# A differential-attention block on one core: the heads' norm factors go through TensorE transposes instead of DRAM, and GpSimd computes them

## The chip, the cores and the metric

The kernel runs on one core of one Trainium2 chip. The metric is its device time in microseconds (us): of one run, from start to end on the chip. A core has five engines that each work through an instruction queue of their own in order: TensorE (PE, whose weight loads are listed as PEld), VectorE (DVE), ScalarE (ACT), GpSimd (POOL) and SyncE (SP), which here mostly issues DMAs. They wait for each other by semaphores.

## The reference, cut to what matters

One layer of a hybrid block on a sequence of 1024 rows of 1024 values: a normalised input is projected, one branch is an mLSTM, the other a differential attention of 8 heads; both are gated, projected, mixed and added. The change touches the end of the attention. Of head `h`:

```python
p = jax.nn.softmax(scores, axis=-1)
p_diff = p[:, :, 0] - lam * p[:, :, 1]
att = jnp.einsum('bhqk,bkhd->bqhd', p_diff, v)
...
att = rmsnorm(att, da_subln_g[layer]) * (1.0 - lambda_init)
y_b = att.reshape(B, S, DA_WIDTH).astype(x.dtype) * jax.nn.silu(b_z)
```

`rmsnorm` divides each row (a query position) by the root of the mean square of its 128 values. So there is one factor per head and row, 1024 factors per head.

## The kernel before, in words

All products are made in parts: each fp32 operand is split into a high and a low part (`wH`, `wL`, `hH`, `hL`, `pH`, `pL`), and three products are summed. The program runs through an opening, the mLSTM's projections, the attention, the mLSTM and the output passes. In the attention, a head has eight blocks of 128 query rows, numbered `t`:

- `scores` (line 906 on): PE writes two score maps of 128x1024 into the S banks (L919). DVE takes the negative maximum `nm` (L922), ACT the exponentials `e` with their sums `Z` (L924), DVE combines the two (`r`, `e`, L928 to L930).
- `transposes` (T): PE turns the 128x128 blocks of `e` four at a time into the one T bank (L131, a helper that records every transpose), ACT copies the high part `pH` out (L943), DVE the low part `pL` (L944). Then the bank is free again.
- `pv` (PV): 12 products per unit of `pH`, `pL` with `vH`, `vL` (L955), two units per pair of blocks; ACT copies the result, transposed (128 features by 256 rows), to `att` (L957).
- `squares` (M): two transposes of `att` into the PV bank; ACT sums the squares into `ms`, a column per block (L967). After the fourth, that is, at the end of a head, DVE and GpSimd compute the factors `rs`, 128 rows by 8 blocks: `zz` (L971), then the helper `rsqrt` (L141 to L146), in which GpSimd takes the power -0.5 (L142) and DVE the rest with one Newton step, and a last scaling (L973). The tiles have the names `rb_v`, `rb_y`, `rb_w`. GpSimd multiplies `att` with the gate `g` (tile `zg`, L976).
- `finish` (F) and `spread`: `att` has features on its partitions and rows along the free axis, so a row's factor has to be there for all partitions. PE turns `rs` into 8x128 (L131, PV bank), ACT copies it to a tile `rb` (L986), SP stores it to DRAM (`rsd`, L988) and loads it back to all 128 partitions for four blocks (512 rows) at a time (`rb`, L994).
- `scale` (G): DVE multiplies `zg` with the gain and `rb` (L998), SP stores the result (`yb`, L999). G of the first half starts the spread of the second.

While PE works on these, it has other products to fill in: the projections of the next head (`da_proj`: rotary queries and keys, `pj`, L424, whose results go through DVE (L847 to L859), GpSimd (L860 to L864), ACT (L863) and a trip through DRAM, `stk` (L868), into `qq` and `kst` (L870), which the next head's scores read), the gate `z` (L876, L877), the value projections (L446, with `vH`, `vL`, L898 and L899) and gate columns. Their weights `raw` are loaded by SP, cast by ACT (L188, L199) and split by GpSimd (L189, L204).

Who comes when on PE is set by the `Weaver`: it takes units of work from two lists, the attention's units of a head in the order of `da_cycle` and the filling projections, and puts next the unit that can start first by an estimated clock. Units say which others must have ended and how long before (`after`, with the numbers of `LAG` in us), and how long they hold a bank (`hold`). PE's order is kept as written; the other engines' orders are made from it by a scheduler at build time. `z`'s last piece of each half waits in this estimate for G of the head before, since `zg` has two buffers.

## Time and profile before

| | before |
|---|---|
| median of three runs | 1824.18 us (1822.41 to 1827.65) |
| the profiled execution | 1825.16 us |
| its span, first to last instruction | 1823.1 us |
| granted TensorE clock, mean over the span | 0.968 |
| instructions | 25192 |
| matmuls | 9375 |

A row of the busy times gives for each engine the us in which it worked, its share of the span and the count of its instructions. A row of waits reads: engine and line that waited, who ended the wait, us in total, how often, the longest. A row of the timeline reads: start (us from the span's start), duration, engine, line, operation, out<-in, shapes, count, and in brackets the engine's idle time before it and what ended that. `SPq` is a DMA's issue in SP's queue, not its transfer. A matmul's duration includes its way through the array, and matmuls overlap: what one costs PE is the distance between two starts.

### The profile page before, as it was taken

The page shows a single profiled execution, that of the slowest core. Times are in us where ns is not written, and L with a number is a line of the kernel's source. Part 1 is how long each engine was busy: PE and PEld are TensorE (multiplying, and loading weights), DVE is VectorE, ACT ScalarE, POOL GpSimd, SP SyncE. Part 2 cuts the span into 40 slices and gives each one's busy share as a digit, 9 for nine tenths or more (in the row PEclk, how much of TensorE's full clock was granted, in tenths as well). Part 3 has the DMA queues.
Part 4 walks back from the last instruction along what each step waited for, and adds up shares of the span by engine and source line. Part 5 has one row for each costly group of instructions (what it writes and reads, how often), then busy time and mean ns, then how long its engine had stood idle before and what let it go on. Part 6 is the DMA issues. An engine that isn't in the chain of part 4 may idle for free. (4 is left out here: it accounts for less than half of the span.)

```text
span 1823.1 us, 25192 instructions
## 1 busy us (share of the span) xinstructions
PE 1680.3 (92%) x9375; PEld 1398.9 (77%) x9375; DVE 1008.8 (55%) x1855; ACT 781.3 (43%) x1562; POOL 591.3 (32%) x608
## 2 busy tenths in 40 slices
PE   7999999999997978989797979999999989999998
PEld 5787887878776856777576757779989977788887
DVE  5687778751765646555564645522666663216533
ACT  6455555441543434443343435432556554213211
POOL 4866676643313122312231231122123212122100
PEclk9999999999998998989898989999999999999999
DMA  5343443533224113220322132226454426534222
GB/s 172 89 130 116 150 135 117 156 114 116 87 87 133 31 41 121 86 76 15 124 72 91 36 106 73 64 64 202 153 158 143 141 74 208 167 106 160 97 83 87
DMA packets 184973, 199.77 MB, mean 110 GB/s; under 512 B 11225, under 2 KB 134514, under 8 KB 184850
## 3 DMA queue, kind: packets, MB, share of 16 engines
q1 hardware_dynamic: 183938, 196.58, 34.3%
q8 instruction: 73, 1.20, 0.3%
q10 hardware_dynamic: 912, 1.59, 0.2%
q14 instruction: 50, 0.41, 0.1%
HBM read 135.08 MB, written 63.05 MB: 109 GB/s over the span
## 5 line engine op out<-in xcount | busy, mean ns | idle before, releaser
L424 PE MATMUL pj<-hH,wH 128*128 128x512 f32 x640 | 270.5, 423 | 3.8 <-DVE hl L859 1.9
L424 PE MATMUL pj<-hH,wL 128*128 128x512 f32 x640 | 254.4, 397 | 1.8 <-POOL wL L202 1.8
L424 PE MATMUL pj<-hL,wH 128*128 128x512 f32 x640 | 254.1, 397 | 0.2 <-DVE hL L575 0.2
L924 ACT ACTIVATE e<-S,nm 128x1024 f32<-128x1024 f32 x128 | 143.0, 1117 | 138.5 <-DVE nm L922 137.8
L204 POOL TENSOR_TENSOR wL<-raw,wH 128x1024 fp32r<-128x1024 f32 x41 | 101.1, 2465 | 307.4 <-ACT wH L199 293.8
L131 PE MATMUL T<-ident,e 128*128 128x128 f32 x512 | 83.0, 287 | 93.3 <-DVE pL L944 93.1
L944 DVE TENSOR_TENSOR pL<-T,pH 128x512 fp32r<-128x512 f32 x128 | 88.1, 688 | 135.2 <-ACT pH L943 134.8
L922 DVE TENSOR_REDUCE nm<-S 128x1 f32<-128x1024 f32 x128 | 150.5, 1218 | 20.1 <-PE S L919 19.0
L424 PEld LDWEIGHTS pj<-hH,wH 128*128 128x128 f32 x640 | 123.4, 193 | 41.6 <-issue 16.9
L446 PE MATMUL pj<-wH,hH 128*128 128x256 f32 x512 | 150.5, 294 | 0.3
L131 PEld LDWEIGHTS T<-ident,e 128*128 128x128 f32 x512 | 62.1, 146 | 115.3 <-DVE pL L944 107.7
L446 PE MATMUL pj<-wL,hH 128*128 128x256 f32 x512 | 145.5, 284 | 1.4 <-POOL wL L202 1.4
L424 PEld LDWEIGHTS pj<-hH,wL 128*128 128x128 f32 x640 | 122.6, 191 | 31.1 <-POOL wL L202 3.2
L446 PE MATMUL pj<-wH,hL 128*128 128x256 f32 x512 | 145.2, 284 | 0.0
L424 PEld LDWEIGHTS pj<-hL,wH 128*128 128x128 f32 x640 | 123.6, 193 | 20.0 <-DVE hL L575 0.6
L424 PE MATMUL pj<-sl_yb,wH 128*128 128x512 f32 x384 | 121.9, 397 | 4.4 <-ACT sl_yb L1326 1.9
L943 ACT CAST pH<-T 128x512 fp32r<-128x512 f32 x128 | 74.9, 585 | 108.3 <-PE T L131 107.1
L919 PE MATMUL S<-kst,qq 64*128 64x512 f32 x768 | 119.9, 448 | 0.2 <-ACT e L924 0.2
L189 POOL TENSOR_TENSOR wL<-raw,wH 128x512 fp32r<-128x512 f32 x32 | 41.3, 1303 | 205.4 <-ACT wH L188 194.0
L199 ACT CAST wH<-raw 128x1024 fp32r<-128x1024 f32 x56 | 58.8, 1050 | 106.6 <-PE pj L424 92.0
L446 PEld LDWEIGHTS pj<-wH,hH 128*128 128x128 f32 x512 | 98.7, 193 | 4.9 <-issue 3.9
L446 PEld LDWEIGHTS pj<-wL,hH 128*128 128x128 f32 x512 | 98.3, 192 | 2.3 <-POOL wL L202 2.3
(357 smaller groups left out, 4168.3 us busy)
## 6 DMA issues: line engine op xcount, KB each, us to landing
raw<-in_w_in_dram SPq DMA_DIRECT2D x88, 512.0 KB
stk<-hl SPq DMA_DIRECT2D x64, 256.0 KB
qq<-stk SPq DMA_DIRECT2D x16, 512.0 KB
kst<-stk SPq DMA_DIRECT2D x16, 512.0 KB
x<-in_x_dram SPq DMA_DIRECT2D x8, 512.0 KB
cak<-y SPq DMA_DIRECT2D x16, 256.0 KB
cakH<-cin SPq DMA_DIRECT2D x16, 256.0 KB
cakL<-tz SPq DMA_DIRECT2D x16, 256.0 KB
```

What stands on the lines that cost most here:

```text
L131: self.t.transpose(out, in_, self.ident[0:k, 0:k])
L189: self.p.tensor_tensor(out=vw(wL), in0=src, in1=vw(wHf), op=ALU.subtract)
L199: self.a.copy(wH, raw)
L204: self.p.tensor_tensor(out=wL, in0=raw, in1=wHf, op=ALU.subtract)
L424: self.t.matmul(ps, lhsT=l[:, k, :], rhs=r, start=(n == 0), stop=(n == 23))
L446: self.t.matmul(ps[:, i, :], lhsT=l, rhs=r[:, k, :], start=(kh == 0 and k == 0 and m == 0), stop=(kh == 1 and k == 3 and m == 2))
L919: self.t.matmul(ps[:, o], lhsT=qq[r, x, c], rhs=k[r, y, o], start=(m == 0), stop=(m == 2))
L922: v.tensor_reduce(out=nm, in_=ps, axis=AX.X, op=ALU.max, negate=True)
L924: a.activation(out=e, in_=ps, func=AF.Exp, bias=nm[:, 0:1], accum_out=Z[:, j, t:t + 1])
L943: a.copy(pH[:, :, s], ps)
L944: v.tensor_tensor(out=pL[:, :, s], in0=ps, in1=pH[:, :, s].bitcast(F32), op=ALU.subtract)
```

## The change

The trip through DRAM goes: `finish` and `spread` are removed, and with them the unit F, the tile `rb` and its DMAs. Instead `scale` (G) becomes a unit of PE that takes the T bank. For each of its four blocks it transposes one column of `rs`, read 128 times over by a broadcast access pattern, so that the 128 factors of the block stand along the free axis on every partition. DVE multiplies from that bank. The whole chain of `rs` is done by GpSimd, where a fused multiply-add of two tensors becomes two instructions. In `da_cycle` G moves from t = 4 and 6 to t = 4 and 5. In `LAG`, F is now how long G comes after the last M (6.0), and G, the time from G to the last piece of `z`, is 6.0 for both halves (it was 18.9 and half of that). The end of the last head is woven anew with one unit less.

```diff
-LAG = dict(Th=2.2, Sh=5.0, PVh=3.7, Mh=8.1, Fh=5.0, qk=14.0, T=6.8, PV=3.7, M=4.5, F=0.4, TTh=1.9, TT=3.2, POh=1.6,
-           PO=1.7, Wh=0.3, W=2.0, STh=2.1, ST=4.9, th=1.8, t=4.1, aq=9.0, outh=6.6, out=14.0, G=18.9)
+LAG = dict(Th=2.2, Sh=5.0, PVh=3.7, Mh=8.1, qk=14.0, T=6.8, PV=3.7, M=4.5, F=6.0, TTh=1.9, TT=3.2, POh=1.6,
+           PO=1.7, Wh=0.3, W=2.0, STh=2.1, ST=4.9, th=1.8, t=4.1, aq=9.0, outh=6.6, out=14.0, G=6.0)
...
-    def rsqrt(self, pool, ssq, scale, bias, name, bufs=1):
+    def rsqrt(self, pool, ssq, scale, bias, name, bufs=1, eng=None):
...
+        v = eng or self.v
...
-            self.v.scalar_tensor_tensor(out=val, in0=ssq, scalar=scale, in1=bias, op0=ALU.mult, op1=ALU.add)
+            if eng is None:
+                v.scalar_tensor_tensor(out=val, in0=ssq, scalar=scale, in1=bias, op0=ALU.mult, op1=ALU.add)
+            else:
+                v.tensor_scalar(out=val, in0=ssq, scalar1=scale, scalar2=None, op0=ALU.mult)
+                v.tensor_tensor(out=val, in0=val, in1=bias, op=ALU.add)
         self.p.tensor_tensor(out=y, in0=val, in1=self.mhalf[:, 0:shp[1]], op=ALU.pow)
-        self.v.tensor_tensor(out=w, in0=y, in1=y, op=ALU.mult)
+        v.tensor_tensor(out=w, in0=y, in1=y, op=ALU.mult)
...
-            z[(half + 1) * self.PIECES - 1].after = ((("G", h - 1, half), LAG["G"] / (half + 1)),)
+            z[(half + 1) * self.PIECES - 1].after = ((("G", h - 1, half), LAG["G"]),)
...
-                v.scalar_tensor_tensor(out=zz, in0=Z0, scalar=EPS, in1=Z0, op0=ALU.mult, op1=ALU.mult)
-                rs = self.rsqrt(w1, st["ms"], 1.0 / 128.0, zz, "rb")
-                v.tensor_scalar(out=rs, in0=rs, scalar1=(1.0 - LAMBDA_INIT) * 0.5, scalar2=None, op0=ALU.mult)
+                p.tensor_scalar(out=zz, in0=Z0, scalar1=EPS, scalar2=None, op0=ALU.mult)
+                p.tensor_tensor(out=zz, in0=zz, in1=Z0, op=ALU.mult)
+                rs = self.rsqrt(w1, st["ms"], 1.0 / 128.0, zz, "rb", eng=p)
+                p.tensor_scalar(out=rs, in0=rs, scalar1=(1.0 - LAMBDA_INIT) * 0.5, scalar2=None, op0=ALU.mult)
...
-        def finish():
-
-            rs = st["rs"]
-            ps = self.bank("PV")
-            self.tr(ps[0:8, 0:128], rs)
-            rb = w1.tile([128, 512], F32, name="rb", tag="rb", bufs=1)
-            rows = rb[0:8, 0:128]
-            a.copy(rows, ps[0:8, 0:128])
-            st["rsd"] = dr = self.dram.tile([8, 128], F32, name="rsd", tag="rsd", bufs=2)
-            q.dma_start(out=dr, in_=rows)
-            st["rb"] = rb
-            spread(0)
-
-        def spread(half):
-            src = st["rsd"][4 * half:4 * half + 4].rearrange("(o t) c -> o (t c)", o=1).broadcast_to([128, 512])
-            q.dma_start(out=st["rb"], in_=src)
-
         def scale(half):
-            g = st["g", half]
-            v.scalar_tensor_tensor(out=g, in0=g, scalar=self.subln, in1=st["rb"], op0=ALU.mult, op1=ALU.mult)
+
+            g, rs = st["g", half], st["rs"]
+            ps = self.bank("T")
+            for i in range(4):
+                t = 4 * half + i
+                self.tr(ps[:, i * 128:(i + 1) * 128], rs[:, t:t + 1].broadcast_to([128, 128]))
+            v.scalar_tensor_tensor(out=g, in0=g, scalar=self.subln, in1=ps, op0=ALU.mult, op1=ALU.mult)
             q.dma_start(out=self.yb[h][:, half * 512:(half + 1) * 512], in_=g)
...
-            G=lambda half: Unit(0.0, lambda: scale(half), name=("G", h, half)),
-            F=lambda: Unit(TP, finish, tag="PV", hold=LAG["Fh"], after=((("M", h, 3), LAG["F"]),)))
+            G=lambda half: Unit(4 * TP, lambda: scale(half), tag="T", hold=LAG["Th"], name=("G", h, half),
+                                after=((("M", h, 3), LAG["F"]),)))
...
-        if prev and t in (4, 6):
-            un.append(prev["G"](t // 2 - 2))
+        if prev and t in (4, 5):
+            un.append(prev["G"](t - 4))
```

The new file is a few lines shorter, and from `rsqrt` on its lines have other numbers; the rows of the new order below have the new ones (`pL` is L949, `zg` L992, the chain L976 to L979 and L145 to L151).

First DVE, where it scales the first half of head 0, while head 1 is computed. Before:

```order
L944 TENSOR_TENSOR pL<-T,pH 128x4x128
L922 TENSOR_REDUCE nm<-S 128x1 x2
L928 RECIPROCAL r<-Z 128x1
L998 SCALAR_TENSOR_TENSOR zg<-zg,cols,rb 128x512
L929 TENSOR_SCALAR r<-r,Z,nlam 128x1
L944 TENSOR_TENSOR pL<-T,pH 128x4x128
L930 SCALAR_TENSOR_TENSOR e_5196<-e_5200,r,e_5196 128x1024
```

And now:

```order
L949 TENSOR_TENSOR pL<-T,pH 128x4x128
L927 TENSOR_REDUCE nm<-S 128x1 x2
L992 SCALAR_TENSOR_TENSOR zg<-zg,cols,T 128x512
L933 RECIPROCAL r<-Z 128x1
L934 TENSOR_SCALAR r<-r,Z,nlam 128x1
L935 SCALAR_TENSOR_TENSOR e_5185<-e_5189,r,e_5185 128x1024
L904 TENSOR_TENSOR vL<-pj,vH 128x256
L949 TENSOR_TENSOR pL<-T,pH 128x4x128
```

The scaling stands at about the same place behind the reductions, but reads the T bank in place of `rb`; the next `pL` is still behind it.

Second GpSimd, at the end of head 1, while head 2 is computed. Before:

```order
L189 TENSOR_TENSOR wL<-raw,wH 128x8x64 x4
L976 TENSOR_TENSOR zg<-att,zg 128x512
L204 TENSOR_TENSOR wL<-raw,wH 128x1024
L976 TENSOR_TENSOR zg<-att,zg 128x512
L142 TENSOR_TENSOR rb_y<-rb_v,mhalf 128x8
L860 TENSOR_TENSOR m_5886<-m_5886,hl 128x512
```

And now:

```order
L194 TENSOR_TENSOR wL<-raw,wH 128x8x64 x4
L982 TENSOR_TENSOR zg<-att,zg 128x512
L209 TENSOR_TENSOR wL<-raw,wH 128x1024
L982 TENSOR_TENSOR zg<-att,zg 128x512
L145 TENSOR_SCALAR rb_v<-ms 128x8
L146 TENSOR_TENSOR rb_v<-rb_v,zz 128x8
L147 TENSOR_TENSOR rb_y<-rb_v,mhalf 128x8
L148 TENSOR_TENSOR rb_w<-rb_y 128x8
L149 TENSOR_TENSOR rb_w<-rb_w,rb_v 128x8
L150 TENSOR_SCALAR rb_w<-rb_w 128x8
L151 TENSOR_TENSOR rb_y<-rb_y,rb_w 128x8
L979 TENSOR_SCALAR rb_y<-rb_y 128x8
```

The eight instructions of the chain stand where the power alone stood, behind the splits of weights.

Third PE, towards the end of head 2, where the last rotary projection for head 3 ends (`pj_6096` before, `pj_6097` now) and the gate's projection begins (`pj_6179`, `pj_6222`). Before:

```order
L424 MATMUL pj_6096<-hL1_173,wH_5650 128x512
L424 MATMUL pj_6096<-hH1_171,wL_5651 128x512
L424 MATMUL pj_6179<-hH0_170,wH_5794 128x512
L424 MATMUL pj_6179<-hL0_172,wH_5794 128x512
L424 MATMUL pj_6179<-hH0_170,wL_5795 128x512
L955 MATMUL PV_6183<-pH_5968,vH_5252 128x256
```

And now:

```order
L960 MATMUL PV_6156<-pH_6013,vL_5244 128x256
L429 MATMUL pj_6097<-hH1_171,wH_5653 128x512
L429 MATMUL pj_6097<-hL1_173,wH_5653 128x512
L429 MATMUL pj_6097<-hH1_171,wL_5654 128x512
L131 MATMUL T_6187<-ident_146,e0_6038 128x128 x4
```

The projection used to end before the PV products of this place; now these and a group of transposes stand ahead of its last piece.

More of the change, by code (lines that the diff above doesn't have):

```diff
@@ L138, in rsqrt @@
         if isinstance(bias, float):
-            self.v.tensor_scalar(out=val, in0=ssq, scalar1=scale, scalar2=bias, op0=ALU.mult, op1=ALU.add)
+            v.tensor_scalar(out=val, in0=ssq, scalar1=scale, scalar2=bias, op0=ALU.mult, op1=ALU.add)
         else:
-            self.v.scalar_tensor_tensor(out=val, in0=ssq, scalar=scale, in1=bias, op0=ALU.mult, op1=ALU.add)
+            if eng is None:
[3 more added lines that the diff above has]
+                v.tensor_tensor(out=val, in0=val, in1=bias, op=ALU.add)
         self.p.tensor_tensor(out=y, in0=val, in1=self.mhalf[:, 0:shp[1]], op=ALU.pow)
-        self.v.tensor_tensor(out=w, in0=y, in1=y, op=ALU.mult)
-        self.v.tensor_tensor(out=w, in0=w, in1=val, op=ALU.mult)
-        self.v.tensor_scalar(out=w, in0=w, scalar1=-0.5, scalar2=1.5, op0=ALU.mult, op1=ALU.add)
-        self.v.tensor_tensor(out=y, in0=y, in1=w, op=ALU.mult)
+        v.tensor_tensor(out=w, in0=y, in1=y, op=ALU.mult)
+        v.tensor_tensor(out=w, in0=w, in1=val, op=ALU.mult)
+        v.tensor_scalar(out=w, in0=w, scalar1=-0.5, scalar2=1.5, op0=ALU.mult, op1=ALU.add)
+        v.tensor_tensor(out=y, in0=y, in1=w, op=ALU.mult)
         return y
@@ L1032, in da_cycle @@
             un.append(before["T"]((t - 1) % 8, 0))
-        if prev and t == 3:
-            un.append(prev["F"]())
         if before:
@@ L1572, in build @@
                 prev = cur
-            end = sum((self.da_cycle(None, prev, t) for t in range(7)), [])
-            w.weave(end[:-3], fill(2))
+            end = sum((self.da_cycle(None, prev, t) for t in range(6)), [])
+            w.weave(end[:-2], fill(2))
             more, c = fill(1), self.PIECES // 2
-            w.add(*more[:c], end[-3], *more[c:2 * c], end[-2], *more[2 * c:3 * c], end[-1], *more[3 * c:])
+            w.add(*more[:2 * c], end[-2], *more[2 * c:3 * c], end[-1], *more[3 * c:])
             w.add(leave("ps1", "w1", "tab"))
```

3 lines of the change are left out of this document (removed).

## The prediction

> **What bounds the kernel now.** I began with the page: which engine fills the span. In this row stand busy time, share of the span and instructions of each engine.
>
> ```profile
> PE 1680.3 (92%) x9375; PEld 1398.9 (77%) x9375; DVE 1008.8 (55%) x1855; ACT 781.3 (43%) x1562; POOL 591.3 (32%) x608
> ```
>
> PE is the bound, and the other engines matter only where they make it wait. The change lies in the attention, so next I took busy times by stretch, from its first scores product at 457 us to its end at about 1245 us, cut where a head's scores begin. I call the time from a head's first scores to the next head's its stretch; the head before it is finished in it. The stretches of heads 1 and 2 and the sum of all (columns: stretch, length, busy time of PE, PEld, DVE, ACT, POOL, granted clock, DMA share, GB/s).
>
> ```profile
> 526.00:622.00 96.00, 83.80 (x557) 71.30 (x555) 55.37 (x80) 40.49 (x86) 20.99 (x15) 0.91 0.23 72
> 622.00:722.00 100.00, 83.96 (x460) 65.82 (x460) 52.53 (x77) 40.57 (x85) 26.17 (x20) 0.91 0.26 79
> ...
> sum 788.00, PE 690.72 PEld 561.74 DVE 428.50 ACT 330.08 POOL 198.02; mean PE 76.75 PEld 62.42 DVE 47.61 ACT 36.68 POOL 22.00
> ```
>
> Here PE is idle for 788.0 - 690.7 = 97.3 us, and its clock falls to 0.91. The waits of this part say on whom: first PE's list, then DVE's (total us, times, longest).
>
> ```profile
> PE T L131 <- DVE pL L944: 93.1, 33, 10.6
> ```
> ```profile
> DVE zg L998 <- DMA rb<-rsd: 77.5, 16, 10.0
> ```
>
> PE waits to overwrite the one T bank, which DVE has not read out with `pL`. DVE in turn sits in front of `zg`, the scaling with the spread factors, until the DMA has landed. PE's timeline shows how the 93.1 us are made up: six waits of over 10 us, one in each of the stretches 1 to 6, where heads 0 to 5 are finished (first, second and last of the six here).
>
> ```profile
> 588.88 1.12 PE L131 MATMUL T<-ident,e 128*128 128x128 f32 x4 [10.64 <-DVE pL L944]
> ...
> 686.11 1.11 PE L131 MATMUL T<-ident,e 128*128 128x128 f32 x4 [10.09 <-DVE pL L944]
> ...
> 1072.28 1.12 PE L131 MATMUL T<-ident,e 128*128 128x128 f32 x4 [10.10 <-DVE pL L944]
> ```
>
> The six come to 61.5 us (10.64, 10.09, 10.26, 10.11, 10.29, 10.10). For the first of them, DVE's timeline and the DMA issues show the cause.
>
> ```profile
> 587.29 0.75 DVE L998 SCALAR_TENSOR_TENSOR zg<-zg,cols,rb 128x512 f32<-128x512 f32 x1 [8.88 <-DMA rb<-rsd]
> ```
> ```profile
> 568.10 0.29 SPq L988 DMA_DIRECT2D rsd<-rb  x1
> ...
> 572.21 3.87 SPq L868 DMA_DIRECT2D stk<-hl  x4
> 576.19 2.23 SPq L994 DMA_DIRECT2D rb<-rsd  x1
> ```
>
> The factors go to DRAM at 568.1; the spread is issued only at 576.2, behind four `stk` stores in SP's queue, and it has landed at 587.3, 11.1 us later, its packets running beside those of the stores. DVE is in order: `pL` stands behind `zg`, PE's transposes behind `pL`.
>
> A second loss follows each wait. In the windows right behind the six waits, PE is busy throughout at a granted clock of 0.50.
>
> ```profile
> 588.90:595.10 6.20, 6.20 (x27) 4.84 (x28) 4.46 (x7) 0.86 (x2) 0.00 (x0) 0.50 0.66 250
> ...
> 1072.30:1076.30 4.00, 4.00 (x17) 2.65 (x17) 2.33 (x4) 0.59 (x1) 0.00 (x0) 0.50 0.97 304
> sum 28.70, PE 28.68 PEld 20.55 DVE 19.35 ACT 4.49 POOL 0.00; mean PE 4.78 PEld 3.42 DVE 3.23 ACT 0.75 POOL 0.00
> ```
>
> 28.7 us at half rate do 14.35 us of work; the other 14.35 us are lost.
>
> **The change part by part.**
>
> Removed, the way through DRAM. Eight stores and sixteen spreads leave SP's queue, and with them the only thing for which DVE's `zg` waits there. In the new order on DVE `zg` stands behind the two reductions of a scores unit, and PE has issued the four spreading transposes while these ran. So the six waits go, 61.5 us, with the half rate behind them, 14.35 us. For heads 6 and 7 DVE waited too, but PE had projections to do, and I count nothing.
>
> Moved, the chain of the norm factor. Seven small DVE instructions per head go to GpSimd. In the stretches 2, 4, 6 and 7 they cost PE something. Here are DVE, ACT and PE in stretch 2, and PE's last wait of this kind.
>
> ```profile
> 649.38 0.17 DVE L143 TENSOR_TENSOR rb_w<-rb_y 128x8 f32<-128x8 f32 x1 [1.78 <-POOL rb_y L142]
> ...
> 650.77 1.28 DVE L930 SCALAR_TENSOR_TENSOR e<-e,r,e 128x1024 f32<-128x1024 f32 x1
> 651.97 0.68 DVE L944 TENSOR_TENSOR pL<-T,pH 128x512 fp32r<-128x512 f32 x1
> ```
> ```profile
> 648.30 0.20 ACT L924 ACTIVATION_READ_ACCUMULATOR e<-S,nm 128x1 f32 x1
> ```
> ```profile
> 652.71 0.80 PE L131 MATMUL T<-ident,e 128*128 128x128 f32 x4 [3.23 <-DVE pL L944]
> ```
> ```profile
> 1138.84 1.12 PE L131 MATMUL T<-ident,e 128*128 128x128 f32 x4 [3.25 <-DVE pL L944]
> ```
>
> There are four such waits (3.23, 3.23, 3.23, 3.25, 12.9 us in all). Without the chain, DVE could start on `r` when ACT's sum is there, at 648.5. With `r` taking 0.5 us, `e` starts at 649.05 and not at 650.77, 1.7 us earlier, and `pL` with it. So about 1.7 us of each wait goes and 1.5 us stay: 4 x 1.7 = 6.8 us. The half rate behind these four is this.
>
> ```profile
> 653.10:656.50 3.40, 3.40 (x14) 2.35 (x14) 1.44 (x3) 0.59 (x1) 0.00 (x0) 0.50 0.00 0
> ...
> sum 18.10, PE 18.05 PEld 12.49 DVE 6.65 ACT 2.34 POOL 0.00; mean PE 4.51 PEld 3.12 DVE 1.66 ACT 0.59 POOL 0.00
> ```
>
> Its price is 9.05 us. Whether a wait of 1.5 us still brings a half-rate stretch is open; the nearest rows are waits of 2 us, three of which PE has, in the stretches 2, 4 and 6 (first and last), and the clock in the stretch behind the first.
>
> ```profile
> 702.70 0.66 PE L131 MATMUL T<-ident,e 128*128 128x128 f32 x4 [2.02 <-DVE pL L944]
> ...
> 1088.87 0.66 PE L131 MATMUL T<-ident,e 128*128 128x128 f32 x4 [2.24 <-DVE pL L944]
> ```
> ```profile
> 703.00:715.50 12.50, 12.49 (x66) 9.09 (x65) 8.74 (x11) 6.00 (x13) 1.29 (x1) 0.86 0.37 114
> ```
>
> A mean of 0.86 over 12.5 us is 2 x 0.14 x 12.5 = 3.5 us at 0.50, so 2 us of waiting was enough once. I take half of the 9.05, 4.5 us, and keep 0 and 9.05 as ends. The Trainium skill, TensorE: Matmul & The Clock Gate, section Why this matters for your kernels, sets the limit at idle gaps of about 3 us. By that rule the whole 9.05 us come back and the sum gains another 4.5 us; the row above, half rate after 2.02 us, goes against it here.
>
> What the chain costs on GpSimd. Small multiplies are not in the trace. The power of the same 128x8 is, and so are multiplies of 128x512 and 128x1024.
>
> ```profile
> 551.88 1.29 POOL L864 TENSOR_TENSOR hl<-m,hl 128x512 fp32r<-128x512 f32 x1
> 553.70 1.66 POOL L142 TENSOR_TENSOR rb_y<-rb_v,mhalf 128x8 f32<-128x8 f32 x1 [0.53 <-DVE rb_v L141]
> 556.26 2.39 POOL L204 TENSOR_TENSOR wL<-raw,wH 128x1024 fp32r<-128x1024 f32 x1 [0.90 <-ACT wH L199]
> ```
>
> 512 elements more cost 1.10 us, which leaves 0.19 us for nearly none; the upper end is the power's 1.66. The eight instructions from `ms` on thus last 1.66 + 7 x 0.2 = 3.1 us, at most 8 x 1.66 = 13.3 us. I take 3.1. In heads 0 to 6 this is hidden at either end: the power started at 553.7, the old spread's way began at 568.1, and PE's new transposes stand still later in its order. In the last head only 27 projection matmuls lie between, so at 13.3 us PE would wait some 7 us there, once; at 3.1 not at all, and I count nothing. The Trainium skill, GPSIMD Engine Reference, section Key points, speaks against such a move: elementwise work is about twice as fast on the DVE. By that, the seven would take 0.34 us each and the chain 4.0 us, under the same cover; no run here shows it.
>
> Added, PE's work. Sixteen groups of four transposes. A group of `T` starts at 721.30 and the next instruction at 721.89 (rows below), 0.59 us, so 16 x 0.59 = 9.4 us more (a little less for the eight single transposes that go; the broadcast column as weights is not in the trace, and I give it the same price).
>
> Added, a turn of the one T bank per group. PE's next transposes must wait for `zg`. Behind the first group of stretch 1 stand 24 matmuls of value pieces, and DVE reaches `zg` right after its reductions, so I take 0. The upper end is the wait of 2 us above, 3.7 us with its half rate.
>
> Moved, the hand-over to the next head. In the stretches 2, 4 and 6, the new PE order puts the next head's last rotary projection behind 24 matmuls of PV and one group of transposes, which earlier stood between it and that head's first scores. Those scores need it through DVE, GpSimd, ACT and a round trip through DRAM (`stk`, then `qq` and `kst`). The rows for the end of stretch 2: DVE's start, the load's issue, the windows behind it, PE's start, and the first and last of 24 such PV matmuls.
>
> ```profile
> 694.01 0.69 DVE L858 TENSOR_TENSOR hl<-pj,sinT 128x512 f32<-128x512 f32 x1 [1.54 <-PE pj L424]
> ```
> ```profile
> 715.53 0.46 SPq L870 DMA_DIRECT2D kst<-stk  x1
> ```
> ```profile
> 715.50:720.00 4.50, 4.50 (x34) 4.14 (x34) 2.07 (x5) 1.91 (x6) 0.00 (x0) 1.00 0.69 236
> 720.00:722.00 2.00, 1.30 (x9) 0.70 (x8) 0.69 (x1) 1.97 (x3) 0.45 (x1) 1.00 0.00 0
> ```
> ```profile
> 721.30 0.66 PE L131 MATMUL T<-ident,e 128*128 128x128 f32 x4 [0.69 <-DVE pL L944]
> 721.89 1.65 PE L919 MATMUL S<-kst,qq 64*128 64x512 f32 x12
> ```
> ```profile
> 561.46 0.28 PE L955 MATMUL PV<-pH,vH 128*128 128x256 f32 x1
> ...
> 564.16 0.28 PE L955 MATMUL PV<-pH,vL 128*128 128x256 f32 x1
> ```
>
> The data took 720.0 - 694.0 = 26.0 us and PE came after 27.9 us. Now PE comes 2.8 + 0.6 us earlier, after 24.5 us, and if the 2 us wait in this stretch goes with its half rate (3.7 us), after 20.8 us. The first half of the scores (0.8 us) needs only what came before. So PE will wait 0.7 to 4.4 us at three places. With 0.7 the loss is 2 us in all. With 4.4, and 2.3 us of half rate behind it as behind the waits of 3.2 us, less the 3.7 us, it is 3.0 us each, 9 us in all. I take 8, because ACT's new order has the `pH` cast ahead of the casts that held it up.
>
> The sum: 61.5 + 14.35 + 6.8 + 4.5 - 9.4 - 8 = 69.75 us. The profiled execution took 1825.16 us, 1823.1 of it span; that gives 1755.4. The median of the runs is 1.0 us below this execution, so 1754 us is the forecast.
>
> **The rivals.**
>
> All short waits go too. Then the four waits leave whole (12.9 + 9.05), the three of 2 us as well (6.3, with half rate 5.2), and the loads come in time: 61.5 + 14.35 + 12.9 + 9.05 + 11.5 - 9.4 = 99.9 us, 1724 us. For it: DVE has less to do. Against it: `pL` still stands behind `e` in DVE's order.
>
> The bank's turn costs. If each of the 16 groups brings PE a wait of 2 us and its 1.7 us of half rate, 59 us go back, and the time is 1813 us. For it: there is one T bank, and every wait of PE here is for it. Against it: the work placed behind each group.
>
> Slower: the chain is caught in GpSimd's queue. In the stretches 2, 4 and 6 four splits of rotary weights and one more split stand ahead of it, and such splits wait for ACT's cast; GpSimd's list has this.
>
> ```profile
> POOL wL L189 <- ACT wH L188: 190.9, 15, 41.5
> ```
>
> PE reaches the groups no sooner than 14.4 us behind the power's old start (568.1 - 553.7). If a split is held for the longest 41.5 us from there, PE waits 27.1 us and loses 2.4 us by half rate (14.35 / 6): 3 x 29.5 = 88.5 us, 1842 us. It decides from a hold of 14.4 us on, and overturns the gain from about 35 us (70 / 3 - 2.4 + 14.4). Against it: in the run before the splits ahead of the chain were done before the chain's input was.
>
> That DVE goes on waiting for the DMA is excluded, since the built order has no such DMA.
>
> **How the numbers follow.** Forecast 0.70, all short waits gone 0.13, the bank 0.11, the queue 0.06. A measurement of this kernel tells 0.3% (5.5 us) from no change. Faster than that are the first two and most of the third: 0.91. Within it: 0.03, the third's upper end. Slower: 0.06. For the range I go from halfway to the first rival, 1726, upward through the forecast's unknowns (half rate 4.5, last head 7 with 2.4 of half rate, hand-over 1, and the bank's turns at seven of the sixteen groups, 26) to 1795.
>
> **What would show it.** Right: DVE has no wait on a DMA in the attention, PE's waits on `pL` fall from 93.1 to about 20 us, none near 10, and the clock of its stretches rises from 0.91 to 0.95 or more. New should be waits of PE for `kst` at the starts of heads 3, 5 and 7, of 0.7 to 4.4 us. Wrong would be PE waiting on `rb_y` of GpSimd, or on `zg` before the next transposes, by over 2 us each.

## The result, and the profile after

| | before | after |
|---|---|---|
| median of four runs | 1825.62 us (1822.41 to 1827.65) | 1750.64 us (1748.29 to 1753.10) |
| ratio after / before, 95% interval | | 0.9591 (0.957 to 0.9612) |
| the profiled execution | 1825.16 us | 1750.27 us |
| its span | 1823.1 us | 1748.5 us |
| granted TensorE clock, mean over the span | 0.968 | 0.992 |
| matmuls | 9375 | 9431 |

The kernel is 75 us faster, against a forecast of about 70. I read the new profile in the order of the old one. First the row of busy times.

```profile
PE 1664.4 (95%) x9431; PEld 1390.5 (80%) x9431; DVE 990.8 (57%) x1799; ACT 780.6 (45%) x1554; POOL 608.6 (35%) x680
```

PE has 56 matmuls more (64 spreading transposes come, eight single ones go) and yet 16 us less of busy time: at half rate the starts of two 128x512 products lay 427 ns apart in before, at full rate 227 ns (medians). GpSimd has 72 instructions more and 17 us more. Next the attention by stretch (same columns as before: stretch, length, PE, PEld, DVE, ACT, POOL, clock, DMA share, GB/s); the two rows shown are again those of heads 1 and 2.

```profile
526.00:611.00 85.00, 81.33 (x562) 69.94 (x560) 52.01 (x73) 40.28 (x86) 24.42 (x24) 0.98 0.23 73
611.00:698.00 87.00, 81.55 (x461) 64.51 (x460) 51.44 (x70) 39.79 (x83) 27.10 (x28) 0.96 0.29 85
```

They were 96 and 100 us long at a clock of 0.91. Now PE's waits in the attention, and DVE's on `zg`.

```profile
PE T L131 <- DVE pL L949: 36.7, 27, 2.8
...
PE S L924 <- DMA kst<-stk: 0.3, 1, 0.3
```
```profile
DVE zg L992 <- PE T L131: 26.5, 2, 24.0
```

The 77.5 us of DVE's waits on the DMA are gone, and PE's 93.1 us on `pL` are 36.7, none above 2.8. The 26.5 us belong to the last head, where DVE has nothing else to do. What is left for PE are short waits at fixed places; one of each sort from PE's timeline:

```profile
556.34 0.33 PE L131 MATMUL T<-ident,e 128*128 128x128 f32 x1 [1.79 <-DVE pL L949]
...
639.83 0.33 PE L131 MATMUL T<-ident,e 128*128 128x128 f32 x1 [1.53 <-DVE pL L949]
...
683.78 0.47 PE L131 MATMUL T<-ident,e 128*128 128x128 f32 x1 [2.79 <-DVE pL L949]
```

The second sort is what remains of the four waits of 3.2 us: 1.53, 1.50, 1.52 and 1.52. The third stands where the three waits of 2 us stood: 2.79, 2.77, 2.76. The first is new at this size (1.79, 1.75, 1.79 in the stretches 1, 3, 5). Here are ACT and DVE ahead of the 2.79 us.

```profile
678.72 1.12 ACT L929 ACTIVATE e<-S,nm 128x1024 f32<-128x1024 f32 x1 [0.85 <-DVE nm L927]
...
680.11 1.10 ACT L929 ACTIVATE e<-S,nm 128x1024 f32<-128x1024 f32 x1
...
681.20 0.58 ACT L948 CAST pH<-T 128x512 fp32r<-128x512 f32 x1
```
```profile
681.33 0.16 DVE L933 RECIPROCAL r<-Z 128x1 f32<-128x1 f32 x1 [1.52 <-ACT e L929]
681.53 0.27 DVE L934 TENSOR_SCALAR r<-r,Z,nlam 128x1 f32<-128x1 f32 x1
681.84 1.28 DVE L935 SCALAR_TENSOR_TENSOR e<-e,r,e 128x1024 f32<-128x1024 f32 x1
683.04 0.68 DVE L949 TENSOR_TENSOR pL<-T,pH 128x512 fp32r<-128x512 f32 x1
```

`pH` is placed behind both exponentials of the next scores unit, `pL` behind `r` and `e` of it. The three sorts named have this picture. Two others don't: before a head's first scores PE waits 0.75 us, where `pL` waits for `pH` and `pH` for the transposes before, and one wait of 1.91 us (at 1021.1) comes from a `pH` behind casts that wait for GpSimd. Last the chain on GpSimd, in the last head, and PE's first spreading transposes there.

```profile
1150.21 0.23 POOL L145 TENSOR_SCALAR rb_v<-ms 128x8 f32<-128x8 f32 x1 [6.89 <-ACT PV L972]
...
1150.81 1.67 POOL L147 TENSOR_TENSOR rb_y<-rb_v,mhalf 128x8 f32<-128x8 f32 x1
1152.55 0.20 POOL L148 TENSOR_TENSOR rb_w<-rb_y 128x8 f32<-128x8 f32 x1
...
1153.69 0.24 POOL L979 TENSOR_SCALAR rb_y<-rb_y 128x8 f32<-128x8 f32 x1
```
```profile
1155.26 0.60 PE L131 MATMUL T<-ident,rb_y 128*128 128x128 f32 x4
```

From 1150.21 to 1153.93 the chain takes 3.7 us, and PE needs it 1.3 us later.

To compare kernels I split the attention, from the first scores to the first transposes of the mLSTM behind it, into three: PE's idle time; what the half rate costs (half of the time in which PE ran at a granted clock of 0.50); and the rest, PE's work at full rate. By the starts above, half is nearly right: 227 of 427 ns. Each row is worked out from the trace of one execution.

| kernel | attention, us | PE idle | at half rate | its cost | work |
|---|---|---|---|---|---|
| before | 788.0 | 97.4 | 60.5 | 30.2 | 660.3 |
| after | 713.5 | 37.7 | 16.4 | 8.2 | 667.6 |
| chain back on DVE | 742.7 | 55.5 | 42.1 | 21.0 | 666.2 |
| before, chain on GpSimd | 765.7 | 88.7 | 31.0 | 15.5 | 661.4 |
| before, factors on ACT's queue | 752.6 | 62.3 | 59.4 | 29.7 | 660.6 |
| before, both | 734.9 | 54.4 | 39.4 | 19.7 | 660.8 |
| after, transposes twice | 717.3 | 37.5 | 9.9 | 5.0 | 674.9 |
| after, spread in the PV bank | 738.4 | 57.3 | 24.3 | 12.2 | 668.9 |
| after, T between the PV units | 704.8 | 28.1 | 19.5 | 9.7 | 667.0 |

The attention is 74.5 us shorter: 59.7 less idle, 22.0 less lost to the half rate, 7.3 more work. The rest of the program is the same to 0.2 us. In the other kernels of the table the rest is 1.8 to 9.1 us longer than in after, so a kernel's time does not follow from its attention alone.

### The profile page after: what moved, and what is told of

Read it like the earlier page. It is cut to its first block, busy times and chain, and to the rows that moved or that the text cites. A ratio compares the mean times of both kernels' runs of the same rounds, so it can differ in the third digit from the quotient of the medians.

```text
span 1748.5 us, 25290 instructions
## 1 busy us (share of the span) xinstructions
PE 1664.4 (95%) x9431; PEld 1390.5 (80%) x9431; DVE 990.8 (57%) x1799; ACT 780.6 (45%) x1554; POOL 608.6 (35%) x680
## 3 DMA queue, kind: packets, MB, share of 16 engines
q1 hardware_dynamic: 181506, 192.35, 35.4%
## 5 line engine op out<-in xcount | busy, mean ns | idle before, releaser
L949 DVE TENSOR_TENSOR pL<-T,pH 128x512 fp32r<-128x512 f32 x128 | 88.2, 689 | 136.7 <-ACT pH L948 136.6
L131 PE MATMUL T<-ident,e 128*128 128x128 f32 x512 | 78.8, 277 | 36.9 <-DVE pL L949 36.7
L924 PE MATMUL S<-kst,qq 64*128 64x512 f32 x768 | 111.3, 422 | 0.7 <-ACT e L929 0.5
L451 PEld LDWEIGHTS pj<-wH,hL 128*128 128x128 f32 x512 | 97.8, 191 | 0.2
```

The source lines that it names most:

```text
L131: self.t.transpose(out, in_, self.ident[0:k, 0:k])
L451: self.t.matmul(ps[:, i, :], lhsT=l, rhs=r[:, k, :], start=(kh == 0 and k == 0 and m == 0), stop=(kh == 1 and k == 3 and m == 2))
L924: self.t.matmul(ps[:, o], lhsT=qq[r, x, c], rhs=k[r, y, o], start=(m == 0), stop=(m == 2))
L949: v.tensor_tensor(out=pL[:, :, s], in0=ps, in1=pH[:, :, s].bitcast(F32), op=ALU.subtract)
```

## The experiments

Twelve kernels were run, each in four runs beside runs of before on the same chip. Ratios are to before, with a 95% interval. The theory under test is the prediction's: the trip through DRAM made the six long waits, the chain on DVE a part of the four of 3.2 us, and half rate follows waits. Against it stood that one of the two parts of the change does it all, that the place in SP's queue and not the trip is to blame, and that the short waits now left are the price of the T bank's turn or of GpSimd's load.

**The chain alone back on DVE.**

```diff
-                rs = self.rsqrt(w1, st["ms"], 1.0 / 128.0, zz, "rb", eng=p)
-                p.tensor_scalar(out=rs, in0=rs, scalar1=(1.0 - LAMBDA_INIT) * 0.5, scalar2=None, op0=ALU.mult)
+                rs = self.rsqrt(w1, st["ms"], 1.0 / 128.0, zz, "rb")
+                v.tensor_scalar(out=rs, in0=rs, scalar1=(1.0 - LAMBDA_INIT) * 0.5, scalar2=None, op0=ALU.mult)
```

(`zz` goes back to one DVE instruction in the same way.)

> The changed kernel with the chain of rs back on DVE (power alone on GpSimd), the transposes kept. Theory A: the gain comes from DVE no longer waiting for the spread's DMA, the chain's move is a side effect of about 1.7 us at each of the four stretches 2, 4, 6 and 7 plus some half rate. Then this kernel takes 7 to 16 us more than the changed one, 1757 to 1767 us, and PE's waits before T of 3.2 us are back in those four stretches. Rival B: the move of the chain is at least half of the gain. Then 1785 us or more.

Measured 1781.24 us (1779.24 to 1783.92), ratio 0.975 (0.9732 to 0.9769), 29 us above after by the ratios: too far for the first theory, not far enough for the second. The four waits of 3.2 us are back, as expected, but in the stretches 1, 3 and 5 there are also three of 5.65 us. PE, DVE and GpSimd at the first of these:

```profile
560.28 0.47 PE L131 MATMUL T<-ident,e 128*128 128x128 f32 x1 [5.65 <-DVE pL L949]
```
```profile
554.88 0.17 DVE L148 TENSOR_TENSOR rb_w<-rb_y 128x8 f32<-128x8 f32 x1 [1.77 <-POOL rb_y L147]
...
555.49 0.17 DVE L151 TENSOR_TENSOR rb_y<-rb_y,rb_w 128x8 f32<-128x8 f32 x1
555.68 2.25 DVE L978 TENSOR_SCALAR rb_y<-rb_y 128x8 f32<-128x8 f32 x1
557.85 0.15 DVE L933 RECIPROCAL r<-Z 128x1 f32<-128x1 f32 x1
...
559.54 0.68 DVE L949 TENSOR_TENSOR pL<-T,pH 128x512 fp32r<-128x512 f32 x1
```
```profile
555.57 2.34 POOL L209 TENSOR_TENSOR wL<-raw,wH 128x1024 fp32r<-128x1024 f32 x1 [0.72 <-ACT wH L204]
```

In this order the whole chain stands ahead of `r`, `e` and `pL`. DVE loses 1.8 us waiting for the power, and 2 us more in its last tiny instruction: 128x8 took 2.25 us instead of 0.17 and ended with GpSimd's split of weights beside it (557.9). This instruction took 2.25, 2.26 and 2.30 us in the three stretches with the waits of 5.65 us, each time beside such a split, and 0.17 us in the other heads, where no split ran beside it. In after the same `pL` started at 555.60, 3.9 us earlier. The Trainium skill, SBUF — State Buffer, section SBUF: two separate sides, says that GpSimd shares a pair of ports with those DVE instructions that run in a 2-port mode or have two inputs in SBUF, and that the one that comes second is blocked for the other's whole instruction; the two ends at 557.9 agree with it, while no run here shows the mode of this instruction. So taking the chain off DVE removes more than its seven instructions: also a trip to GpSimd and back in the middle of DVE's queue, and a collision.

**Before, the chain alone on GpSimd.** The edit is the diff's part on `rsqrt`, `zz` and the last scaling, and nothing else.

```diff
-                rs = self.rsqrt(w1, st["ms"], 1.0 / 128.0, zz, "rb")
+                rs = self.rsqrt(w1, st["ms"], 1.0 / 128.0, zz, "rb", eng=p)
```

> The kernel before with the chain on GpSimd and the spread still through DRAM. Theory A: the six waits of DVE for rb and of PE for T, 10 us each, stay; the four of 3.2 us fall to about 1.5; 1808 to 1818 us. Rival B: 1787 us or less.

Measured 1808.48 us (1804.73 to 1811.79), ratio 0.9905 (0.9884 to 0.9926): 17 us gained, as expected. The six waits of 10 us stay, the four of 3.2 us become 1.5 (here the first). In the profiled execution's attention, 8.7 us of the gain are idle time and 14.7 us half rate.

```profile
647.91 0.66 PE L131 MATMUL T<-ident,e 128*128 128x128 f32 x4 [1.52 <-DVE pL L949]
```

This settles that the chain was the cause of these four, by 1.7 us each, and that the six do not hang on it; with the way through DRAM gone and the chain on DVE, the run before, they were gone.

**Before, the factors' DMAs from ACT's queue**, so that they don't stand behind the `stk` stores.

```diff
-            q.dma_start(out=dr, in_=rows)
+            a.dma_start(out=dr, in_=rows)
...
-            q.dma_start(out=st["rb"], in_=src)
+            a.dma_start(out=st["rb"], in_=src)
```

> The kernel before, with the store and the two spreads of the factors issued from ACT's queue, all else as it was. It tells which part of the way through DRAM makes DVE wait. Theory A1: the spread lands late because its packets run behind and beside those of the four stk stores, issued just before it from the same queue; from a queue of its own it lands some 3 to 5 us after its issue, the waits of DVE fall from 10 to about 2 us, and 1760 to 1785 us result. Rival A2: it lands late because it is issued late (576 us) and takes its 10 us whatever the queue; then the issue from ACT, which stands behind two casts that wait for GpSimd, is hardly earlier, and the time stays within 1815 to 1835 us.

Measured 1795.51 us (1794.35 to 1798.45), ratio 0.983 (0.9812 to 0.9848), between the two. The queues and DVE in stretch 1, and the sum of DVE's waits:

```profile
573.43 0.34 ACTq L994 DMA_DIRECT2D rb<-rsd  x1
```
```profile
580.75 0.75 DVE L998 SCALAR_TENSOR_TENSOR zg<-zg,cols,rb 128x512 f32<-128x512 f32 x1 [3.24 <-DMA rb<-rsd]
```
```profile
DVE zg L998 <- DMA rb<-rsd: 46.1, 16, 6.1
```

The spread is issued 2.8 us earlier and lands 7.3 us after its issue instead of 11.1. It runs beside the stores all the same (issued here from 572.81 on), and DVE still waits for it. PE's six waits fall from 10 us to 5.0 and 3.3. So the place in SP's queue was a part of the cause; the other is the time of the transfer itself, which the change to ACT's queue didn't take away. How much of it is due to the stores beside it was not tested. In the profiled execution the attention is 35.4 us shorter, but the rest of the program 9 us longer, in idle time and at half rate; why the rest grew stays open.

**Before, both of these.** The two diffs above together.

> The kernel before with both other ways to help DVE: the chain on GpSimd and the spread's DMAs issued from ACT's queue. It asks whether the transposes are needed at all. Theory A: the spread still takes some 9 us beside the stk stores and DVE still waits for it, so the two gains add up, 1827.8 - 32.2 - 19.3 = 1776 us, 1768 to 1784. Rival: with the chain out of DVE's way the factors are ready early enough for the spread to land in time; 1740 to 1756 us, as with the transposes and without their work on PE.

Measured 1776.05 us (1774.93 to 1782.71), ratio 0.9738 (0.9713 to 0.9764). By the ratios the chain alone had brought 17 us and the queue alone 31; together 48 came. In the attention alone (table) it was 22.3 and 35.4 us, and 53.1 together. The 27 us that remain to after, by the ratios, come with the transposes and the order woven around them.

**After, each spreading transpose done twice**, the second over the first.

```diff
+                for _ in range(2):
+                    self.tr(ps[:, i * 128:(i + 1) * 128], rs[:, t:t + 1].broadcast_to([128, 128]))
```

> The changed kernel with each spreading transpose made twice into the same place: 64 more transposes. It prices PE's added work. If PE is the bound throughout the attention and a group costs PE 0.46 to 0.59 us (7.3 us by the attention's sum in the changed kernel, 9.4 us forecast), this takes 7 to 10 us more than the changed one, 1758 to 1761 us. If the groups fall into waits that PE has anyway, less than 3 us more.

Measured 1753.98 us (1753.22 to 1757.14), ratio 0.9604 (0.9586 to 0.9621). By the ratios this is 2 us more than after, less than the 7 expected. In the profiled execution the work of the attention grew from 667.6 to 674.9 us, by 7.3, just as much as the first set (less eight single transposes) had added to before. PE's idle time hides none of it (37.7 and 37.5 us), but the half rate happened to give 3.2 back, and the attention grew by 3.8. A group of four costs PE 7.3 / 16 = 0.46 us.

**After, five more powers at the end of GpSimd's chain** (with ones as exponents, so that the values stay).

```diff
+                for _ in range(5):
+                    p.tensor_tensor(out=rs, in0=rs, in1=self.ones8, op=ALU.pow)
```

> The changed kernel with five more powers (exponent 1, so the factors keep their values) at the end of GpSimd's chain: 5 x 1.67 = 8.3 us more until the factors are ready, in every head. It tests the cover of the chain. In the changed kernel the first head's factors are ready at 556.9 us and PE's first transpose of them starts at 572.7, so 15.8 us are free: by theory A the time stays within 5 us of the changed kernel in heads 0 to 6, and the last head alone may wait some 3 us: 1749 to 1757 us. Rival: GpSimd's other work (rotary parts, weight splits) is on the critical way and 8 us more per head push it: 1765 us or more.

Measured 1768.95 us (1766.64 to 1770.76), ratio 0.9695 (0.9672 to 0.9718): 19 us more than after by the ratios, which is the rival's side. But PE's waits show that heads 0 to 6 took it unchanged, and that one wait came, in the last head.

```profile
PE T L131 <- DVE pL L949: 36.6, 27, 2.8
PE T L131 <- POOL rb_y L981: 9.4, 1, 9.4
```

The 8.3 us of powers and a weight split of 2.34 us that got in between, less the 1.3 us that were free, make 9.4. The attention is 9.5 us longer; in the profiled execution 6.6 us more lie behind the attention. They are PE's own work: in the output passes its products start 232 ns apart (median) instead of the 227 ns of all the other traces. No experiment tells why. They arise long after the chain, so the time alone doesn't bear out the rival. The cover is large everywhere but in the last head, where it is 1.3 us.

**After, the Weaver told that the T bank is held for 3.4 us** and not 2.2, so that it spaces the transposes out.

```diff
-LAG = dict(Th=2.2, ...
+LAG = dict(Th=3.4, ...
```

> The changed kernel with one number of the weave raised: a unit of transposes is taken to hold the T bank for 3.4 us instead of 2.2, so that more other work is put before the next unit on it. PE's remaining waits in the attention are 36.7 us, all before T, of 0.75 to 2.8 us. If they come from units of T set too close for DVE to free the bank, a good part goes: 5 to 25 us less than the changed kernel. If they come from pL standing behind the softmax work in DVE's queue, which more distance hardly helps, within 5 us.

Measured 1810.14 us (1804.41 to 1810.80), ratio 0.9911 (0.9887 to 0.9934): 58 us above after, neither theory.

```profile
PE T L131 <- DVE pL L949: 75.5, 26, 9.7
```

The waits are as many and twice as long, with three of 7.1 to 9.7 us. The estimate's number moves every unit behind it, not only the one it names; it is no measure of what the bank costs.

**After, the splits of the rotary weights on DVE**, to see whether GpSimd, which makes `m`, holds ACT up ahead of `pH`.

```diff
-                self.p.tensor_tensor(out=vw(wL), in0=src, in1=vw(wHf), op=ALU.subtract)
+                self.v.tensor_tensor(out=vw(wL), in0=src, in1=vw(wHf), op=ALU.subtract)
```

> The changed kernel with the splits of the rotary weights (four of 1.3 us per head on GpSimd) on DVE. In the stretches 2, 4 and 6 the last two of them stand in GpSimd ahead of the rotary parts m, for which ACT's cast waits, and pH behind that cast: the 2.8 us waits of PE. Theory A: with the splits gone from GpSimd m comes 2.5 us earlier, the three waits fall to 1 us or less and the loads of kst come earlier too: 4 to 10 us less than the changed kernel. Rival: DVE, with 2.8 us more per head, frees T later, and the time stays or rises by up to 10 us.

Measured 1751.15 us (1750.59 to 1751.54), ratio 0.9594 (0.9577 to 0.9612), no change. The loads of `kst` at the ends of the stretches 2, 4 and 6 are issued 2.6, 1.1 and 0.5 us earlier, and the three waits stay (2.70, 2.70, 2.77). GpSimd's splits of these weights are not their cause.

**After, the first group of transposes ahead of the scores in every second cycle.**

```diff
-            un.append(before["T"]((t - 1) % 8, 0))
+            un.insert(0 if cur and t % 2 == 0 else len(un), before["T"]((t - 1) % 8, 0))
```

> The kernel after, with the first group of transposes of a block put ahead of the next scores unit in every second cycle. Theory A: the waits of 1 to 3 us that are left (37 us in all) come from the order on DVE, where pL stands behind the two reductions, r and e of the scores unit that was put ahead of the transposes. Then the waits of the even cycles go or shrink, PE's wait on pL falls from 36.7 us to under 25, and the time is 1732 to 1745. Rival B: pL is late because ACT's pH is late whatever the order, or the scores, put later, make their e late: the waits stay or grow, 1748 or more.

Measured 1780.54 us (1775.20 to 1783.52), ratio 0.9754 (0.9721 to 0.9787), 30 us worse. PE's waits on `pL` are fewer, 19, but sum to 52.0 us, with one of 7.4 and several of 3 to 4.5. That the scores come later, and with them their `e`, is the likely reason, not a tested one. As an order it is worse; of the two theories it tells nothing, since everything behind it was woven anew.

**After, the first group of transposes between the two PV units in the other cycles.**

```diff
-            un.append(before["T"]((t - 1) % 8, 0))
+            un.insert(len(un) - 1 if own and t % 2 == 1 else len(un), before["T"]((t - 1) % 8, 0))
```

> The kernel after, with the first group of transposes put between the two PV units in the odd cycles, so that it has 12 PV products more behind it before the second group. Theory A (order on DVE decides, a fixed time from scores to pL): more work of PE between the two groups covers 2.8 us of each wait in odd cycles; PE's wait on pL falls by 5 to 15 us and the time is 1733 to 1746. Rival B: the estimate by which the order is made spaces the groups out anyhow, and the waits stay: 1747 to 1755.

Measured 1743.79 us (1743.52 to 1745.32), ratio 0.9559 (0.9537 to 0.958). That is 6 us below after by the ratios, whose intervals just overlap. PE's waits on `pL`:

```profile
PE T L131 <- DVE pL L949: 27.7, 27, 3.0
```

They are 9 us less, with the same work. That DVE reaches `pL` a fixed time after the scores, and that 12 products between the two groups of transposes let PE arrive later, was the theory, and the waits went its way. This supports the reading of the DVE and ACT rows above without proving it. It is the fastest version of the study.

**After, the spread factors in the PV bank, with the Weaver told so.**

```diff
-            ps = self.bank("T")
+            ps = self.bank("PV")
...
-            G=lambda half: Unit(4 * TP, lambda: scale(half), tag="T", hold=LAG["Th"], name=("G", h, half),
+            G=lambda half: Unit(4 * TP, lambda: scale(half), tag="PV", hold=LAG["Fh"], name=("G", h, half),
```

> The kernel after, with the spread factors written to the PV bank and not to the T bank, so that no transposes of e wait for the scaling. Theory A: the turn of the T bank costs nothing, as the sum had it: within 4 us of the kernel after (1747 to 1755). Rival B: the waits of 1.1 to 1.8 us that are new in the kernel after come from this turn: 8 to 14 us less (1737 to 1743).

Measured 1807.41 us (1802.06 to 1810.20), ratio 0.9902 (0.9874 to 0.993), 57 us worse, outside both theories. The Weaver put G elsewhere, and ACT shows what followed, in three stretches:

```profile
698.46 0.60 ACT L881 ACTIVATE zg<-pj 128x512 f32<-128x512 f32 x1 [9.85 <-DMA yb<-zg]
698.95 0.58 ACT L948 CAST pH<-T 128x512 fp32r<-128x512 f32 x1
```

The next gate wants a `zg` buffer whose store to `yb` isn't out yet; ACT waits, `pH` stands behind it, PE waits 10.3 us for `pL` (13.3 and 6.1 in the other two). This says nothing of the bank, so I made the test again with the order kept.

**The same, but PE's order left as in after** (the Weaver still counts G to the T bank).

```diff
-            ps = self.bank("T")
+            ps = self.bank("PV")
```

> The kernel after with the spread factors in the PV bank, while the planner still counts them to the T bank, so that PE's order stays as in the kernel after, instruction by instruction. Theory A: the turn of the T bank costs nothing there, as the sum had it: within 4 us of the kernel after (1747 to 1755), and the waits of 1.1 to 1.8 us stay. Rival B: these waits come from the turn of the T bank: 8 to 14 us less (1737 to 1743).

Measured 1777.54 us (1775.60 to 1778.46), ratio 0.9741 (0.9717 to 0.9765), 27 us worse. PE's waits:

```profile
PE T L131 <- DVE pL L949: 37.2, 27, 3.1
PE PV L131 <- ACT PV L972: 11.5, 3, 3.8
PE PV L960 <- DVE zg L992: 8.1, 7, 1.2
```

With the same order and another bank, the 27 waits for the T bank are what they were (36.7 us in after). So the spread's turn of the T bank causes none of them. In the PV bank it costs 11.5 + 8.1 = 19.6 us of waits instead, and 4.0 us more of half rate.

## Why the prediction was right, and where its sizes were off

The mechanism held: the six waits were the trip through DRAM, the four the chain on DVE, and both are gone or shortened as worked out. That the sum came within 5 us is in part luck: single terms were off by up to 9 us, both ways. Term by term (gains are positive):

| term | forecast, us | measured | from |
|---|---|---|---|
| the six waits | 61.5 | 61.5 | none above 2.8 us is left |
| half rate behind them | 14.35 | 14.35 | no 0.50 at these places |
| the four waits, 3.2 to 1.5 us | 6.8 | 6.9 | 12.94 less (1.53 + 1.50 + 1.52 + 1.52) |
| half rate behind the four | 4.5 | 9.05 | no 0.50 behind any of the four |
| PE's transposes | -9.4 | -7.3 | work 660.3 to 667.6 |
| hand-over to the next head | -8 | -3.7 | see below |
| the last head's wait for `rs`, and half rate behind it | 0 | 4.3 | 2.61 + 1.71, see below |
| new or longer short waits elsewhere | 0 | -9.0 | rest of the idle time |
| half rate behind one of these | 0 | -1.7 | 3.4 us at 0.50 from 898.2 on |
| sum | 69.75 | 74.4 | 74.5 by the table of kernels |

**Half rate behind the four.** I took half of 9.05, the nearest row being a wait of 2.02 us with a slowed stretch behind it. The whole came back. The last section shows why 1.5 us is not near 2.

**Transposes.** I took the distance of 0.59 us from a group of T to the next instruction; that distance holds the change from transposes to other matmuls too. 0.46 us is what a group adds.

**Hand-over.** This is the step that failed. I took 8 us "because ACT's new order has the `pH` cast ahead of the casts that held it up": the waits of 2 us would go, PE would come at the next scores earlier, and wait there for the data. PE does wait there, but for 0.3 us in all. DVE's start, the load's issue and PE's start at the end of stretch 2:

```profile
671.96 0.68 DVE L863 TENSOR_TENSOR hl<-pj,sinT 128x512 f32<-128x512 f32 x1
```
```profile
693.76 0.46 SPq L875 DMA_DIRECT2D kst<-stk  x1
```
```profile
698.42 0.96 PE L924 MATMUL S<-kst,qq 64*128 64x512 f32 x6
```

From DVE's start PE came after 26.5 us. The forecast had 24.5 with the wait of 2 us and 20.8 without it. The wait didn't go, it grew to 2.8 us, since `pH` now stands behind two exponentials (rows above) instead of behind casts. I had read in the order what no longer stood ahead of `pH` and not what now did. The three waits rose by 2.0 us together, 0.3 us came for `kst`, and the half rate behind them rose from 3.4 to 4.8 us: 3.7 us. (In before only two of the three waits had half rate behind them, so the 5.2 us with which the first rival counts is 3.4.)

**The last head's wait.** The prediction saw no cost of the new chain there and counted nothing. But in before PE had waited there for the old chain:

```profile
1225.13 0.27 PE L131 MATMUL PV<-ident,rb_y 128*8 128x128 f32 x1 [2.61 <-DVE rb_y L973]
```

Half rate from 1226.5 on cost 1.71 us more. In after PE doesn't wait there, and none of its half rate lies there: a gain of 4.3 us without a term.

**The bank's turn.** Taken as 0, rightly: the kernel with the PV bank and the same order shows the same 27 waits. The short waits that are new, 1.79 us and others, come by the rows above from the order of `pH` and `pL` behind the next scores, which the weaving made anew. I had no term for them, and with 9.0 us they are the largest miss of the sum. For the same reason PE's waits on `pL` came to 36.7 us, where the forecast's sign was about 20; its other signs came as said, but for the waits for `kst`. The new places of G and the new numbers of `LAG` were not tested by themselves.

**The chain on GpSimd.** Forecast 3.1 us, measured 3.7: instructions of 0.20 to 0.24 us, as the extrapolation gave, and 0.08 us between dependent ones, which I hadn't counted. The estimate by the rate of the Trainium skill (GPSIMD Engine Reference, section Key points) had been 4.0. It was hidden in all heads, but in the last by 1.3 us only; the five powers show what lies behind that. Counting it at nothing was right here, by little.

**The chain's worth.** As a term of the sum it was 11.3 us (6.8 + 4.5). Alone in the old order it brought 17. In the new order its absence costs 29, since the scheduler there places it ahead of `pL` as a whole, beside a weight split. Transposes with the chain on DVE bring 46 us (1 - 0.975), the chain alone 17, both together 75. The parts don't add up, though in the time those of the queue and the chain did.

The rivals are refuted by the rows shown: short waits are left (against the first), none is due to the bank (the second), and PE never waits on `rb_y` in after (the third). The range's lower end is not what its words say: halfway from 1754 to 1724 is 1739, not 1726. The measured 1750.64 lies above both.

## What to carry to other kernels

A small transfer that another engine waits for in order costs more than its bytes (here 11.1 us from issue to use): take it off the DMA path if PE has a cheap way (here 0.46 us per 512 factors on each partition), and only then look at queues. Before counting on a wait to go, look in the new order for what now stands ahead of the instruction that ends it, on each engine of its chain. Where a program sets the order by estimates, test a suspected cost with the order kept; a change of the estimates tests another order (here 58 us for one number).

## What the runs showed of the hardware

**The half rate is decided in steps.** In all ten traces that I laid beside each other, half-rate stretches begin on a grid: in after at 526.1, 683.1, 898.2 and 1027.9, which are 0, 46.0, 109.0 and 147.0 steps of 3.413 us. The Trainium skill, TensorE: Matmul & The Clock Gate, section What's actually happening, gives this window, 3413 ns and free-running, and the traces agree. The Trainium skill, section Why this matters for your kernels of the same page, wants idle gaps below about 3 us; here shorter ones were enough, by where they fell. Rows of after, a step each, with PE's busy time as the first number behind the comma and the granted clock third from the end: the step in which the wait of 2.77 us ended, three other steps with idle time, and the three right behind these.

```profile
853.78:857.20 3.42, 2.17 (x15) 1.64 (x17) 2.48 (x4) 0.59 (x1) 1.28 (x1) 1.00 0.65 204
```
```profile
553.41:556.82 3.41, 1.62 (x11) 1.08 (x9) 2.86 (x6) 1.97 (x4) 2.96 (x6) 1.00 0.26 84
...
679.70:683.11 3.41, 1.29 (x6) 0.75 (x4) 1.82 (x5) 2.57 (x8) 0.00 (x0) 1.00 0.27 71
...
894.74:898.15 3.41, 1.61 (x10) 1.00 (x11) 3.20 (x6) 1.63 (x2) 3.00 (x7) 1.00 0.26 86
```
```profile
556.82:560.23 3.41, 3.41 (x21) 2.30 (x20) 2.26 (x4) 0.59 (x1) 2.46 (x2) 1.00 0.26 99
...
683.11:686.52 3.41, 2.74 (x9) 2.00 (x11) 1.90 (x4) 0.59 (x1) 1.28 (x1) 0.50 0.63 195
...
898.15:901.56 3.41, 3.41 (x14) 2.29 (x15) 1.27 (x2) 0.00 (x0) 1.52 (x1) 0.50 0.26 102
```

With PE idle for 2.12 us of a step the next one ran at 0.50. With 1.8 us idle it did once and once not (898.15 and 556.82). The wait of 2.77 us that ended at 855.0 fell on two steps, 1.55 and 1.22 us, and nothing followed. In the attention of ten traces (before, after, the chain on DVE or GpSimd, ACT's queue, transposes twice, 3.4 us, T between, and both with the PV bank) 87 full-rate steps were followed by half rate, all with 1.75 us or more of idle time, and 1929 were not, all with 1.94 us or less. The upper bound holds for the rest of these programs too (from 20 us on), the lower one doesn't: behind the attention five drops came after steps with only 1.14 to 1.62 us of idle time. So in the attention a lone wait of 1.5 us brought no half rate, those of 2 to 3.3 us did or didn't, and small shifts of the whole program changed its sum by some us, as in the kernel with the transposes done twice. What decides between 1.75 and 1.94 us, and behind the attention, I didn't find.

**A tiny DVE instruction can take as long as GpSimd's.** With the chain on DVE, the last scaling of 128x8 took 0.17 us where no weight split ran on GpSimd, and 2.25 to 2.30 us in the three heads where one had just begun.
